# A two-block network on one core: priority for weight splits in two stages, one projection moved ahead by a pair of heads, and norm sums placed behind two of four value blocks

## The chip, the cores and the metric

The kernel runs on one core of one Trainium2 chip. The metric is the device time of one execution in microseconds. Of the kernel before, three executions were timed: 2271.51, 2273.09 and 2273.24 us, median 2273.09 us.

TensorE is called PE here (PEld is its loading of weights), VectorE DVE, ScalarE ACT, GpSimd POOL and SyncE SP. SP issues the loads of weights.

## The reference

512 tokens of width 1024 go through four mixers and two feed-forward parts, all in 32-bit floats:

```python
x = x + lru_mixer(rms_norm(x, g0))     # 2x1536 projections, conv of 4 taps, gates, scan, w_out
x = x + fox_mixer(rms_norm(x, g1))     # 16 heads of 64, causal softmax with a forget term
x = rms_norm(x, final_g)
for i in range(2):                     # hybrid layers
    h = rmsnorm(x, norm_mix[i])
    cb, cc, cu, q, k, v, g, ga, gb = split(h @ w_in[i])
    y_conv = (cb * conv3(cc * cu)) @ w_conv_out[i]
    y_ret = (silu(g) * groupnorm(retention(rotary(q), rotary(k), v))) @ w_ret_out[i]
    x = x + (sigmoid(ga) * y_conv + sigmoid(gb) * y_ret) @ w_o[i]
    h2 = rmsnorm(x, norm_mlp[i])
    x = x + square(relu(h2 @ w_up[i])) @ w_down[i]
out = rms_norm(x, norm_final)
```

## The kernel before, in words

**Products.** Activations lie transposed in SBUF: 8 tiles of 128 features by 512 tokens. Every 32-bit operand is split into a high part H (a cast to fp32r on ACT) and a rest L (a subtraction on DVE), and a product is three matmuls, H·H, H·L and L·H (`mm3`, L279 to L281). A projection of 128 columns (`proj`) is 8 times `mm3`, so 24 matmuls of 512 columns.

**Weights.** `Stream` holds a list of weight items in the order of use. `next()` hands out an item and emits the load and the split of the item two places further on (one, where the current item is a pair of up weights). `_emit` takes a raw buffer (4 of them), issues the load on SP (L119), casts on ACT (L60) and subtracts on DVE (L61) into H and L buffers (3 each). For pairs of up weights `_emit_sums` also forms sums of halves (S1, S2, S4) with DVE additions and splits them into 3 small buffers; one pair of up tiles is then seven products of half width (`pair`) in place of eight.

**Order.** PE runs in the order in which the code is written. The order on ACT, DVE, POOL and SP is made by a planner that plays the program through: of the instructions that it thinks ready, it takes the one traced first. A block `high_priority(300)` counts its instructions as traced 300 instructions earlier, and blocks inside each other add up. The order is fixed in the program; on the chip an engine waits at an instruction that isn't ready, with all that is queued behind it.

**LRU stage (0 to 253.6 us).** For n = 0 to 11: `lru_proj(n)` runs the projections xb and gt; inside a priority block it scales xb by the norm row (xbp, L558), convolves it (one ACT and three DVE instructions, L560 and L562) and splits the result into xcH and xcL. `lru_gates(n-1)` multiplies these with two small weights (psr, psi). For each two n `lru_tail` runs the gate functions on ACT, with four loads of function tables (L585, L595, L599, L610), then the scan (L616), and splits y into yH and yL. `lru_out` (lo) multiplies y with the output weights: one chunk in each of n = 7 to 10, the rest at the end.

**Forgetting attention (fox, to about 552 us).** The heads go in 8 pairs. `fox_q(p)` and `fox_k(p)` project (fq, fk) and split into Tq, Tb, k1 and k2, one buffer each; `fox_sc(p, hh)` computes scores and softmax of one head, `fox_tr` transposes the probabilities (pt) and splits them into ptH and ptL, `fox_pv` multiplies with the values (po), `fox_g` projects the gate (fgt). The loop L869 to L880 runs for p = 1 to 7 the scores of pair p-1 among the projections of pair p; only fq of pair 1 is projected ahead of the loop.

**Retention, in each hybrid layer.** For head 0, PE runs rq and rk together (`proj2`), then the sums of squares over the features (`colsum`, cs) that `first_rows` needs for the norm row r; `rot` rotates q and k with r in the cosines and splits them (rqH to rkL). Four value blocks follow (rv, 24 matmuls of 256 columns each), the transposes of r (rc), the gates (rg; in layer 0 ahead of rc), then the scores (rs).

**Up and down.** After the product with w_o, whose results `PairNorm` turns into x tiles and sums for `pair` (xH, xL, TH, TL), four groups of four pairs of up tiles and eight down tiles (dn) follow. PE starts dn on 6 of 8 tiles aH, aL for two outputs, then does the last two.

Of the kernel before, what the change touches and what calls it, by code (L numbers as in the profile page):

```python
# [15 lines left out]
P = 128  # L16
# [32 lines left out]
class Stream:  # L49


    def __init__(self, tc, raw, hi, lo, items, ahead):
        self.nc, self.raw, self.hi, self.lo = tc.nc, raw, hi, lo
        self.items, self.ahead = items, ahead
        self.done, self.taken = [], 0
        self.sums = self.sraw = None
        self.pooled = 0
# [83 lines left out]
    def prefetch(self, upto):  # L141
        while len(self.done) < min(len(self.items), upto):
            if self.items[len(self.done)][1] is None and self.sums is None:
                return
            self._emit()

# [20 lines left out]
def build(tc, A, out, dbg=None):  # L167
# [3 lines left out]
    with ctx:  # L171
# [39 lines left out]
        for i in range(3):  # L211
            add(f"fox_vf{i}", 0, 3 if i < 2 else 2, 256 + FOX_H)
        add("fox_w_in", 24, KD, P)
        for p in range(1, 8):
            for t in (0, 1, 3):
                add("fox_w_in", t * 8 + p, KD, P)
            if p % 2 == 0:
                for kh in range(2):
                    add("fox_v", (p // 2 - 1) * 2 + kh, 4, 256)
# [294 lines left out]
        with ExitStack() as lc:  # L514
# [34 lines left out]
            st, yH, yL = {}, {}, {}  # L549

            def lru_proj(n):
                ps = proj(psum(f"xb{n}"), W.next()) if n > 1 else (ps0, ps1)[n]
# [105 lines left out]
            lru_out(2, (0, 1, 2), nrm)  # L658
            lru_out(2, (3,), nrm)
            if dbg:  # L660
                for j in range(KD):
                    nc.sync.dma_start(dbg["x1"][:, j], x[:, j])
# [4 lines left out]
        with ExitStack() as lc:  # L667
# [201 lines left out]
            for p in range(1, 8):  # L869
                fox_sc(p - 1, 0)  # L870
                fox_q(p, psq if p == 1 else None)
                fox_sc(p - 1, 1)
                fox_tr(p - 1, 0)
                fox_k(p)
                fox_tr(p - 1, 1)
                fox_pv(p - 1, 0)
                fox_g(p)
                fox_pv(p - 1, 1)
                if p % 2 == 0:
                    fox_v(p // 2)  # L880
# [85 lines left out]
        for li in range(2):  # L966
# [3 lines left out]
            with ExitStack() as lc:  # L970
# [74 lines left out]
                for h in range(RET_H):  # L1045
# [3 lines left out]
                    if h == 0:  # L1049
                        ps, psk = proj2((psum(f"rq{li}_{h}"), psum(f"rk{li}_{h}")), (W.next(), W.next()), [(0, 6), (6, 8)])  # L1050
                        r, r0 = first_rows()
                    else:
                        ps = proj(psum(f"rq{li}_{h}"), W.next())
                    qH, qL = rot("rq", h, ps)
                    if prev:
                        prev = head_o(*prev)
                    kH, kL = rot("rk", h, psk or proj(psum(f"rk{li}_{h}"), W.next()))
                    (h0, l0), (h1, l1) = W.next(), W.next()
                    pss = []
                    for tb in range(4):  # L1060
                        ps = psum(f"rv{li}_{h}_{tb}")[:, :256]
                        cs = slice(tb * P, (tb + 1) * P)
# [59 lines left out]
            with ExitStack() as lc:  # L1122
# [48 lines left out]
                lay = ExitStack()  # L1171
                W.sums = lay.enter_context(tc.tile_pool(name=f"u{li}_s", bufs=3, side="right"))
                W.sraw = lay.enter_context(tc.tile_pool(name=f"u{li}_r", bufs=2, side="right"))
                for j in PAIRS:
# [4 lines left out]
            with ExitStack() as lc:  # L1179
# [6 lines left out]
                for g in range(4):  # L1186
                    ah = []
                    for f in range(0, 8, 2):
# [4 lines left out]
                        for i in range(2):  # L1193
# [5 lines left out]
                            split(aH, aL, t)  # L1199
                            ah.append((aH, aL))  # L1200
                    head = [(W.next(), psum(f"dn{li}_{g}_{j}")) for j in range(2)]
                    for ks in (range(6), range(6, 8)):
# [124 lines left out]
```

## Time and profile before

| | |
|---|---|
| median of three executions | 2273.09 us |
| the profiled execution, its own time | 2273.16 us |
| its span | 2271.4 us |
| PE busy | 2213.1 us (97%) |
| PEld busy | 1908.8 us (84%) |
| DVE busy | 1512.9 us (67%) |
| ACT busy | 1087.9 us (48%) |
| POOL busy | 228.0 us (10%) |

The profiled execution has the time of the median, and 1.8 us of it lie outside the span. Busy time of PE counts each matmul from its start to its modelled end, and these overlap; so idle time is a lower bound on what PE lost, and the distance between the starts of successive matmuls tells more. The granted clock of PE is 1.00 when it runs at 2.4 GHz and 0.50 at 1.2 GHz.

### The profile page before, as it was taken

How to read it: one execution, taken by the hardware profiler on the slowest of the kernel's cores; microseconds unless marked ns; L12 is line 12 of the kernel's file. 1: busy time of each engine (PE TensorE's matmuls, PEld its weight loads, DVE VectorE, ACT ScalarE, POOL GpSimd, SP SyncE). 2: the span in 40 equal slices, each digit the busy share in tenths (PEclk: the TensorE clock that was granted, in tenths of full speed). 3: DMA queues.
4: the chain of work that ended last, by engine and by line, in shares of the span. 5: the costliest groups of instructions: out<-in, count | busy, mean ns of one | idle time of the engine just before them, and what ended most of it. 6: DMA issues, size and time to landing. Idle time of an engine off the chain costs nothing.

```text
span 2271.4 us, 29981 instructions
## 1 busy us (share of the span) xinstructions
PE 2213.1 (97%) x11818; PEld 1908.8 (84%) x11818; DVE 1512.9 (67%) x2316; ACT 1087.9 (48%) x1661; POOL 228.0 (10%) x174
## 2 busy tenths in 40 slices
PE   8899999999999999999899999999999999999998
PEld 6677778887988888888898998988888888898997
DVE  7867877778776445548776785676345548786774
ACT  7667567775655222226443444556222236443443
POOL 0324111110111000000110110211000000110111
PEclk9999999999999999999999999999999999999999
DMA  4223312222232333232333333222333232333331
GB/s 156 72 82 106 93 64 67 74 66 93 78 95 75 102 94 101 93 102 82 97 101 94 111 103 99 91 95 75 102 97 99 93 102 83 103 103 102 96 110 56
DMA packets 62940, 210.40 MB, mean 93 GB/s; under 512 B 6992, under 2 KB 11984, under 8 KB 62800
## 3 DMA queue, kind: packets, MB, share of 16 engines
q1 hardware_dynamic: 59984, 204.43, 28.5%
q10 hardware_dynamic: 2672, 3.81, 0.6%
q8 instruction: 92, 1.51, 0.3%
q14 instruction: 48, 0.39, 0.1%
q0 software_dynamic: 144, 0.26, 0.1%
HBM read 206.37 MB, written 2.10 MB: 92 GB/s over the span
## 4 chain that ended last, share of the span: by engine, by line
PE 87%; DVE 7%; ACT 4%; issue 1%; POOL 0%; DMA 0%; DVEq 0%; SPq 0%; ACTq 0%; POOLq 0%
PE dn L281 5%; PE dn L279 5%; PE dn L280 5%; PE up L281 4%; PE up L279 4%; PE up L280 4%; PE ro L1026 1%; PE gb L279 1%; PE gb L281 1%; PE wo L280 1%; PE cu L281 1%; PE cc L281 1%; PE cb L281 1%; PE wr L281 1%; PE wc L280 1%
## 5 line engine op out<-in xcount | busy, mean ns | idle before, releaser
L60 ACT CAST wh<-wr 128x1024 fp32r<-128x1024 f32 (+1 forms) x335 | 337.6, 1010 | 684.1 <-PE dn L280 117.2
L61 DVE TENSOR_TENSOR wl<-wr,wh 128x1024 fp32r<-128x1024 f32 (+1 forms) x335 | 396.1, 1185 | 43.1 <-ACT wh L60 40.7
L279 PE MATMUL dn<-aH,wh 128*128 128x512 f32 x488 | 190.0, 389 | 0.0
L281 PE MATMUL dn<-aH,wl 128*128 128x512 f32 x488 | 189.9, 389 | 0.0
L280 PE MATMUL dn<-aL,wh 128*128 128x512 f32 x488 | 189.9, 389 | 0.0
L439 POOL TENSOR_TENSOR s_up<-s_up,sz_up 128x256 f32<-128x256 f32 x32 | 61.7, 1929 | 1052.2 <-ACT s_up L437 540.7
L1214 DVE TENSOR_TENSOR x<-dn,x 128x512 f32<-128x512 f32 x61 | 42.0, 688 | 104.6 <-PE dn L281 104.6
L281 PEld LDWEIGHTS dn<-aH,wl 128*128 128x128 f32 x488 | 91.6, 188 | 19.1
L280 PEld LDWEIGHTS dn<-aL,wh 128*128 128x128 f32 x488 | 91.6, 188 | 18.8
L279 PEld LDWEIGHTS dn<-aH,wh 128*128 128x128 f32 x488 | 91.6, 188 | 18.8
L280 PE MATMUL rv<-wl,xH 128*128 128x256 f32 x256 | 73.0, 285 | 0.0
L279 PE MATMUL rv<-wh,xH 128*128 128x256 f32 x256 | 73.0, 285 | 0.0
L281 PE MATMUL rv<-wh,xL 128*128 128x256 f32 x256 | 73.0, 285 | 0.0
L1196 ACT ACTIVATE c_up<-c_up 128x512 f32<-128x512 f32 x64 | 40.3, 633 | 26.3 <-DVE c_up L1195 25.4
L281 PE MATMUL rg<-xH,wl 128*128 128x512 f32 x128 | 49.9, 390 | 0.1
L279 PE MATMUL xb<-xH,wh 128*128 128x512 f32 x96 | 40.5, 422 | 9.8 <-ACT wh L60 9.8
L279 PEld LDWEIGHTS rv<-wh,xH 128*128 128x128 f32 x256 | 49.7, 194 | 0.3
L279 PE MATMUL rg<-xH,wh 128*128 128x512 f32 x128 | 49.9, 390 | 0.0
L280 PEld LDWEIGHTS rv<-wl,xH 128*128 128x128 f32 x256 | 49.6, 194 | 0.4
L279 PE MATMUL gb<-xH,wh 128*128 128x512 f32 x128 | 49.9, 390 | 0.0
L280 PE MATMUL rg<-xL,wh 128*128 128x512 f32 x128 | 49.9, 389 | 0.0
L281 PE MATMUL gb<-xH,wl 128*128 128x512 f32 x128 | 49.8, 389 | 0.0
(1549 smaller groups left out, 6960.3 us busy)
## 6 DMA issues: line engine op xcount, KB each, us to landing
wr<-in_w_in SPq DMA_DIRECT2D x112, 512.0 KB, 3.5
wr<-in_w_down SPq DMA_DIRECT2D x64, 512.0 KB, 3.5
wr<-in_fox_w_in SPq DMA_DIRECT2D x24, 512.0 KB, 3.5
wr<-in_lru_w_in SPq DMA_DIRECT2D x22, 512.0 KB, 3.6
wr<-in_w_v SPq DMA_DIRECT2D x16, 512.0 KB, 3.4
wr<-in_w_ret_out SPq DMA_DIRECT2D x16, 512.0 KB, 3.5
wr<-in_w_conv_out SPq DMA_DIRECT2D x16, 512.0 KB, 3.4
wr<-in_w_o SPq DMA_DIRECT2D x16, 512.0 KB, 3.5
```

What stands on the lines that cost most here:

```text
L60: self.nc.scalar.copy(h, src)
L61: self.nc.vector.tensor_sub(l, src, h.bitcast(F32))
L279: pe.matmul(ps, wH, aH, start=start, stop=False)
L280: pe.matmul(ps, wH, aL, start=False, stop=False)
L281: pe.matmul(ps, wL, aH, start=False, stop=stop)
L439: pool.tensor_add(s5, s5, z)
L1026: pe.matmul(po[i][:, q0:], vp[:, kb, vs], sp_[:, so], start=n == 0, stop=n == 11)
L1196: act.activation(t, t, AF.Square)
L1214: dve.tensor_add(x[:, j], ps, x[:, j])
```

## The change

Nothing is added to or taken from the computation: the instructions are the same, in another order.

1. `Stream.prefetch` emits an item inside `high_priority(first)` when `first` is set. It is 300 from the start of the LRU loop to the end of the LRU stage, and in each hybrid layer from the product with w_o to the end of the first group's four up pairs. In `lru_proj` the call of `next()` for gt stands inside a priority block already.
2. In fox, fk of pair p is projected between the scores of the two heads of pair p-1, the gate ahead of the second transposes, and fq of pair p+1 between the two value products. The items are listed in that order. In the last round (p = 7) no fq follows.
3. In retention, head 0, `first_rows` and both `rot` move behind the second of the four value blocks.

```diff
@@ Stream
+        self.tc, self.first = tc, 0
@@ prefetch
-            self._emit()
+            if self.first:
+                with self.tc.high_priority(self.first):
+                    self._emit()
+            else:
+                self._emit()
@@ items
+        add("fox_w_in", 1, KD, P)
         for p in range(1, 8):
-            for t in (0, 1, 3):
-                add("fox_w_in", t * 8 + p, KD, P)
+            add("fox_w_in", 8 + p, KD, P)
+            add("fox_w_in", 24 + p, KD, P)
+            if p < 7:
+                add("fox_w_in", p + 1, KD, P)
@@ LRU
+            W.first = 300
             def lru_proj(n):
...
             lru_out(2, (3,), nrm)
+            W.first = 0
@@ fox
                 fox_sc(p - 1, 0)
-                fox_q(p, psq if p == 1 else None)
+                fox_q(p, psq)
+                psk = proj(psum(f"fk{p}"), W.next())
                 fox_sc(p - 1, 1)
                 fox_tr(p - 1, 0)
-                fox_k(p)
+                fox_k(p, psk)
+                fox_g(p)
                 fox_tr(p - 1, 1)
                 fox_pv(p - 1, 0)
-                fox_g(p)
+                if p < 7:
+                    psq = proj(psum(f"fq{p + 1}"), W.next())
                 fox_pv(p - 1, 1)
@@ retention
                     if h == 0:
                         ps, psk = proj2(...)
-                        r, r0 = first_rows()
                     else:
-                        ps = proj(psum(f"rq{li}_{h}"), W.next())
-                    qH, qL = rot("rq", h, ps)
-                    if prev:
+                        qH, qL = rot("rq", h, proj(psum(f"rq{li}_{h}"), W.next()))
                         prev = head_o(*prev)
-                    kH, kL = rot("rk", h, psk or proj(psum(f"rk{li}_{h}"), W.next()))
+                        kH, kL = rot("rk", h, proj(psum(f"rk{li}_{h}"), W.next()))
...
                     for tb in range(4):
+                        if h == 0 and tb == 2:
+                            r, r0 = first_rows()
+                            qH, qL = rot("rq", h, psh)
+                            kH, kL = rot("rk", h, psk)
@@ up
+                W.first = 300
                 for j in PAIRS:
...
+                    W.first = 0
                     head = [(W.next(), psum(f"dn{li}_{g}_{j}")) for j in range(2)]
```

## Rows read from the trace of the kernel before

**Rows 1.** Timeline of PE at full clock: start, duration, instruction.

```profile
14.87 0.39 PE L281 MATMUL gt<-xH,wl 128*128 128x512 f32 x1
...
24.39 0.39 PE L281 MATMUL xb<-xH,wl 128*128 128x512 f32 x1
```

**Rows 2.** Windows: stretch, length, busy time (instructions) by engine, PE clock, DMA.

```profile
25.30:214.00 188.70, 172.25 (x717) 137.20 (x716) 142.05 (x173) 127.97 (x177) 53.71 (x29) 0.96 0.28 85
214.00:253.60 39.60, 35.31 (x150) 27.69 (x150) 32.44 (x42) 26.71 (x38) 7.69 (x4) 1.00 0.27 83
297.32:304.14 6.82, 4.69 (x16) 3.93 (x17) 6.12 (x21) 5.10 (x17) 1.28 (x1) 0.50 0.00 0
...
552.00:592.00 40.00, 36.77 (x200) 31.69 (x200) 34.39 (x51) 24.38 (x31) 3.08 (x2) 0.96 0.23 73
...
1069.00:1119.00 50.00, 43.59 (x326) 42.26 (x326) 44.25 (x77) 29.48 (x47) 10.10 (x4) 0.93 0.26 85
1917.00:1967.00 50.00, 44.85 (x355) 43.38 (x354) 46.85 (x81) 31.62 (x50) 8.30 (x4) 1.00 0.28 94
```

**Rows 3.** Waits of PE, whole span: total us, times, longest us.

```profile
PE xb L279 <- ACT wh L60: 9.8, 2, 6.1
PE xb L281 <- DVE wl L61: 5.3, 4, 2.9
PE psr L280 <- DVE xcL L305: 5.0, 4, 1.8
...
PE pt L814 <- ACT pr L802: 4.2, 1, 4.2
PE lo L281 <- DVE wl L61: 3.1, 3, 1.7
...
PE gt L281 <- DVE wl L61: 1.7, 2, 1.2
```

**Rows 4.** Timeline of ACT in the LRU stage.

```profile
81.46 1.28 ACT L595 ACT_TABLE_LOAD   x1
...
89.96 1.03 ACT L60 CAST wh<-wr 128x1024 fp32r<-128x1024 f32 x1
```

**Rows 5.** DVE by line, LRU stage and whole: counts; min/median/max ns.

```profile
L61 DVE TENSOR_TENSOR wl<-wr,wh x45: 414/1217/2311, 25.6 to 252.0; 128x1024 fp32r<-128x1024 f32 x33, 128x256 fp32r<-128x256 f32 x12
...
L562 DVE SCALAR_TENSOR_TENSOR xc<-xbp,vec,xc x36: 741/748/1784, 31.6 to 207.7; 128x512 f32<-128x512 f32 x36
```

**Rows 6.** Timeline of PE, first pair of heads; in brackets idle before, releaser.

```profile
299.45 2.50 PE L814 MATMUL pt<-ident,pr 128*128 128x128 f32 x10 [4.18 <-ACT pr L802]
```

**Rows 7.** Timeline, second transposes of fox's last round and their last split.

```profile
491.04 1.25 PE L814 MATMUL pt<-ident,pr 128*128 128x128 f32 x10
...
495.85 0.69 DVE L822 TENSOR_TENSOR ptL<-pt,ptH 128x512 fp32r<-128x512 f32 x1 [0.18 <-ACT ptH L821]
```

**Rows 8.** Timeline of PE, then of DVE, retention of layer 0, head 0.

```profile
592.10 0.48 PE L279 MATMUL rs<-rqH,rkH 128*128 128x512 f32 x1
...
587.62 0.68 DVE L305 TENSOR_TENSOR rkL<-rark,rkH 128x512 fp32r<-128x512 f32 x1
```

**Rows 9.** Timeline of PE, then of DVE, retention of layer 1, head 0.

```profile
1420.54 0.39 PE L335 MATMUL cs_x<-csl_x,ones 128*128 128x512 f32 x1
...
1432.29 0.60 PE L461 MATMUL rc_s<-ident,r_x 128*128 128x128 f32 x4
...
1443.63 0.39 PE L279 MATMUL rs<-rqH,rkH 128*128 128x512 f32 x1
...
1424.56 0.69 DVE L326 SCALAR_TENSOR_TENSOR r_x<-rst_x,r_x 128x512 f32<-128x512 f32 x1
...
1436.18 0.68 DVE L305 TENSOR_TENSOR rkL<-rark,rkH 128x512 fp32r<-128x512 f32 x1
```

**Rows 10.** Timeline of PE, then of DVE, end of the first up group, layer 0.

```profile
1115.54 0.40 PE L279 MATMUL dn<-aH,wh 128*128 128x512 f32 x1
...
1118.26 1.30 DVE L305 TENSOR_TENSOR aL<-c_up,aH 128x512 fp32r<-128x512 f32 x2 [0.23 <-ACT aH L304]
```

More of the change, by code (lines that the diff above doesn't have):

```diff
@@ L1050, in build @@
                         ps, psk = proj2((psum(f"rq{li}_{h}"), psum(f"rk{li}_{h}")), (W.next(), W.next()), [(0, 6), (6, 8)])
-                        r, r0 = first_rows()
                     else:
-                        ps = proj(psum(f"rq{li}_{h}"), W.next())
-                    qH, qL = rot("rq", h, ps)
-                    if prev:
+                        qH, qL = rot("rq", h, proj(psum(f"rq{li}_{h}"), W.next()))
                         prev = head_o(*prev)
-                    kH, kL = rot("rk", h, psk or proj(psum(f"rk{li}_{h}"), W.next()))
+                        kH, kL = rot("rk", h, proj(psum(f"rk{li}_{h}"), W.next()))
                     (h0, l0), (h1, l1) = W.next(), W.next()
                     pss = []
+                    psh = ps if h == 0 else None
                     for tb in range(4):
+                        if h == 0 and tb == 2:
+                            r, r0 = first_rows()
+                            qH, qL = rot("rq", h, psh)
+                            kH, kL = rot("rk", h, psk)
                         ps = psum(f"rv{li}_{h}_{tb}")[:, :256]
```

## The prediction

> **What bounds the kernel now.** The busy table comes first: PE is busy 97% of the span, so the time is PE's and the other engines count only where PE waits for them. Then I ask how fast PE can go: at full clock 42 matmuls of 512 columns in a row start between 14.87 and 24.39 us, 9.52 / 42 = 0.227 us from one start to the next [rows 1]. The windows by stage then show where PE is slower than that [rows 2]. In the LRU loop, 25.3 to 214.0 us, 717 matmuls would take 717 x 0.227 = 162.8 us and took 188.7: 25.9 us lost. In the end of that stage, 214.0 to 253.6, 150 matmuls would take 34.1 of 39.6: 5.5 lost. Fox loses at its first pair of heads, retention of layer 0 in 552 to 592 (3.2 us idle, clock 0.96), and the two first up groups 6.4 and 5.2 us of idle [rows 2]. Everywhere else PE is never idle for long; nothing is to be gained there.
>
> The list of PE's waits says for whom [rows 3]. In the LRU stage it is mostly the splits of weights: xb waits 9.8 us for casts, of which the 6.1 is the start of the program that no order changes, and 5.3 for the subtractions; gt waits 1.7, lo 3.1. The gates wait 5.0 us in four places for xcL, which is no weight. Beside the waits there is the clock: it was 0.96 in the mean over the LRU loop, so 0.04 x 188.7 = 7.5 us went there [rows 2], after stalls of some 3 us. So a long stall is paid for more than once.
>
> **The change, part by part.** No instruction is added, so each part is worth what it takes from these losses, less what is late next.
>
> *Splits first, LRU.* One stall shows the mechanism: the cast at 89.96 stands on ACT behind three table loads and the functions between them, from 81.46 on [rows 4], and xb starts 3.7 us late for it. With priority the cast goes ahead as soon as its raw data are there; then the subtraction, then the next load on SP (each load waits for a raw buffer that a subtraction frees). What can be gained is 3.7 + 5.3 us of waits of xb, 1.7 of gt, the clock's 7.5, and 2.7 that are left of the 25.9 when these and xcL's 5.0 are taken off (PE filling again after stalls): 20.9 us. I don't take all. DVE is busy 142 of 188.7 us; squeezed into 168 that is 85%, with bursts, and the conv chain that is now behind the splits feeds the gates. Each split put ahead of it costs a DVE instruction of 1.2 us [rows 5] and a cast of 1.03 [rows 4]. The gates already wait at 4 of the 12, and xcL of a later n stood behind the same ACT functions, so once PE arrives earlier it will wait there. I take two thirds: **-14** (bounds -4, the waits for xb's casts alone, and -20.9).
>
> *Splits first, end of LRU.* lo waits 3.1 us for weights, but y of the last two n comes at the end of a chain through the gate functions; PE arriving earlier waits for that. **-0.5** (bounds -3.1 to +3: two splits of 1.2 us put ahead of that chain, and some).
>
> *Fox, first pair.* PE stands 4.18 us for the softmax, since both scores follow each other and the transposes come at once [rows 6]; and from 299.45 to 304.14 it runs at half clock [rows 2], 4.7 us of which half is lost. With fk between the two scores (24 x 0.227 = 5.4 us) the softmax of head 0 is covered; the split of that weight is not on the path, since fk and fq of pair 1 keep their places in the list. 4.2 + 2.35 = **-6.5** (bounds -4.2, -7). Rounds 2 to 6 keep the same distances between scores, transposes and value products, with gate and query in exchanged roles: 0. If their cover were gone, each would cost a part of the 4.18.
>
> *Fox, last round.* There fq is missing, so the second value product follows the first at once. The second transposes end at 492.3, their last split at 496.5 [rows 7], 4.2 us later, of which the first value product, 8 matmuls, covers about 1.4. But k's copies, which stood in between, now come earlier. **+1.5** (bounds 0 and 2.8, or 4.5 if the clock falls for it).
>
> *Retention, layer 0.* The sums wait 3.2 us and 0.04 x 40 = 1.6 go by the clock [rows 2]; behind two value blocks the split sums are ready, so 4.8 us go. What is late next: the scores rs began at 592.10, 3.8 us after rkL ended at 588.30 [rows 8]. PE comes 4.8 us earlier there, and the sums themselves end some 1.7 us later than now (two value blocks of 5.5 us in place of waits of 3.2), with the whole chain of r, cosines, rotations behind them on DVE and POOL: 4.8 + 1.7 - 3.8 = 2.7 us of new wait, less if two weight splits ahead of rkL move up. I take 1.2 of it: **-3.6** (bounds -4.8, -2.1).
>
> *Retention, layer 1.* Nothing waits now. The sums come about 5.8 us later, half of the 11.75 us from 1420.54 to 1432.29. r ended 4.7 us after its sums (1425.25), so it is there in time for the transposes; rkL ended at 1436.86 and is needed at 1443.63, 6.8 us of slack against 5.8 of delay [rows 9]. **+0.5** (bounds 0, +3).
>
> *Splits first, up groups.* DVE is busy 44.25 and 46.85 of 50 us there [rows 2], so priority adds no room: it can only push work behind the start of dn. In layer 0 dn began at 1115.54 and needs its last two tiles 36 matmuls later, at 1123.7; they were ready at 1119.56 [rows 10]: 4.1 us can be pushed, and DVE's 5.7 us of idle in this window hold another 2, since part of them is PE at half clock. Lost now are 6.4 idle and 0.07 x 50 = 3.5 by the clock. I take **-5** (bounds 0, -9.9), and for layer 1, with 5.2 idle and no clock loss, half: **-2.5** (bounds 0, -5.2).
>
> *New stalls.* The planner makes its order anew, and the trace of before can't show where that puts an instruction in the way. I add one stall of the longest kind seen, **+4.2** [rows 6].
>
> Sum: -14 - 0.5 - 6.5 + 1.5 - 3.6 + 0.5 - 5 - 2.5 + 4.2 = -25.9 us. From 2273.16, the profiled execution (which stands at the median, 2273.09), this gives **2247**.
>
> A rule that speaks against the first part: a subtraction of L has two inputs in SBUF, and such instructions pay when POOL reads SBUF at the same time. The row: the same conv instruction takes 0.741 to 1.784 us and a large wl up to 2.311 against 1.217 [rows 5], with POOL busy 53.7 of 188.7 us [rows 2]. The Trainium skill states (SBUF — State Buffer, Who interferes with whom) that the two engines share a port pair as an exclusive lock, and whoever comes second is blocked for the whole instruction. By that rule splits moved into POOL's bursts would cost DVE up to 1 us each; it is the third rival.
>
> **The rivals.**
> *The wait moves to xcL and y.* The conv chain has three ACT and five DVE steps, each of which may now stand behind a split. For it: the gates wait already, DVE has 85% to do. Against: a chain of n has some 16 us, gt, xb, gt of PE, before its gates. The LRU gains nothing: 2247 + 14.5 = 2261.
> *Slower.* The same mechanism, larger: if each of the 11 gates in the loop waits for both splits on DVE (2 x 1.2) and both casts (2 x 1.03), 4.5 x 11 = 49 us, and the clock falls at four of them (half of 6.82 each) [rows 2], 14, against 20.9 + 3.1 saved: +39, with the other parts at -11.4: about 2300; it decides from 3.1 us per gate on ((20.9 + 11.4 + 3.1)/11, the clock left aside). Against it speaks that such a stall frees DVE to catch up.
> *The port, and DVE in the up groups.* 33 large splits at up to 1 us, half of it on PE's path, take 8 of the LRU's gain, and up gains nothing: 2247 + 8 + 7.5 = 2262.
> *Priority does nothing,* since a split that waits for its raw data or for a free H buffer can't go earlier whatever its rank: only PE's own reordering counts, -6.5 + 1.5 - 3.6 + 0.5: 2265.
> *More than forecast.* All named losses go, no new stall: 2273.2 - 20.9 - 3.1 - 7 - 4.8 - 15 = 2222.
>
> **How the numbers follow.** Forecast 0.5, the wait at xcL 0.15, slower 0.07, port 0.08, priority without effect 0.12, more than forecast 0.08. The forecast's own bounds are about 12 us to both sides, since its large terms (14 and 7.5) are known to half. To leave out no more than 2 in 10 the range goes up to 2265, over three of the rivals, and down to 2232. A measurement can tell about 0.2%, 4.5 us. Faster than that: all but the slower case and a part of priority without effect: 0.88; within: 0.05; slower: 0.07.
>
> **What would show it.** In the profile after: xb's waits for wh and wl gone from PE's list, the casts standing among the table loads; the half-clock stretches at 92, 130, 297, 567 and 1106 us gone; no wait of pt at the first pair; a wait of po in fox's last round of some 1.5 us; rs of head 0, layer 0, waiting for rkL about 1 us; sl of the up weights still waited for, but half as much; psr's wait for xcL larger than 5.0. Wrong would be the prediction if psr's waits pass 20 us, or if xb still waits for splits.

## The result and the profile after

The changed kernel takes 2285.9 us (median), the kernel before 2273.0 beside it: ratio 1.0059, 95% interval 1.0046 to 1.0072. It is slower by 0.6%, where the prediction said 2247 us and faster with 0.88. The profiled execution has a span of 2284.0 us against 2271.4, so 12.6 us have to be found.

PE has the same 11818 matmuls and the same busy time (page of after):

```profile
PE 2213.7 (97%) x11818; PEld 1905.6 (83%) x11818; DVE 1512.1 (66%) x2316; ACT 1088.9 (48%) x1663; POOL 226.8 (10%) x174
```

The stages say where the time went. The table is read from PE's timeline, from the first matmul of one stage's first product to that of the next (fq starts fox, sc its attention, rq retention, ro is head 0's output, wo to dn holds the first up group). The runs described further down stand in the same table, since the comparison by stage is the argument. Each row is one profiled execution, which can lie some us off its kernel's median (that of e3_ret is the fastest of its ten, that of e10_ret_one the slowest):

| kernel | fq starts | sc to rq | rq to ro, layer 0 | wo to dn, layer 0 | wo to dn, layer 1 | span |
|---|---|---|---|---|---|---|
| before | 253.5 | 261.3 | 47.5 | 93.6 | 90.0 | 2271.4 |
| after | 252.6 | 268.8 | 53.5 | 93.6 | 89.9 | 2284.0 |
| e1_priority | 253.2 | 261.1 | 47.6 | 93.4 | 89.8 | 2270.6 |
| e2_fox | 252.1 | 268.8 | 48.1 | 89.8 | 91.4 | 2275.7 |
| e4_fox_hold | 251.3 | 261.0 | 48.2 | 92.5 | 92.6 | 2271.1 |
| e5_round1 | 252.1 | 257.8 | 47.2 | 89.9 | 91.1 | 2263.6 |
| e3_ret | 251.1 | 260.6 | 53.6 | 91.3 | 91.1 | 2273.2 |
| e8_ret_sin | 252.3 | 261.7 | 50.2 | 91.3 | 89.8 | 2270.9 |
| e10_ret_one | 255.8 | 261.3 | 46.3 | 92.6 | 91.2 | 2272.8 |
| e11_both | 252.3 | 258.2 | 46.2 | 92.8 | 91.3 | 2266.5 |
| e6_lru | 254.7 | 261.8 | 47.3 | 92.4 | 91.3 | 2273.0 |
| e9_bufs | 264.6 | 260.8 | 48.6 | 90.2 | 89.4 | 2281.4 |
| e12_lru2 | 252.2 | 261.3 | 47.5 | 93.5 | 89.6 | 2269.9 |
| e13_lru2_dve | 246.1 | 261.7 | 47.4 | 93.8 | 90.0 | 2264.6 |
| e14_best | 252.2 | 257.8 | 48.3 | 90.0 | 91.2 | 2265.0 |
| e15_all | 246.4 | 257.8 | 47.2 | 91.1 | 89.9 | 2257.9 |
| e16_dve | 243.4 | 262.0 | 47.3 | 92.6 | 91.6 | 2262.4 |
| e17_round1_dve | 243.3 | 257.8 | 47.0 | 91.3 | 91.4 | 2256.3 |
| e18_nopool | 247.2 | 257.8 | 48.2 | 92.8 | 91.3 | 2263.0 |

After minus before: -0.9 to the end of the LRU, +7.5 in fox, +6.0 in retention of layer 0, 0.0 and -0.1 in the up groups, and nothing elsewhere. Some columns also show their own unsteadiness. Kernels with the LRU code of before (before, e2 to e5, e8, e10, e11) end that stage between 251.1 and 255.8. The first up group of layer 0, whose code only the priority touches, takes 89.8 to 90.0 us without a stretch at half clock, 91.1 to 92.8 with one of 3.4 us and 93.4 to 93.8 with one of 6.8 us (e9_bufs, which has other buffers, apart). So a difference of some 4 us between two kernels is read from the stage that was changed, not from the total.

In the LRU the waits of PE, which answer to [rows 3], are nearly what they were; the 6.2 us of psr are no sign of the change, since e2_fox, with the LRU code of before, has 6.4 (after, waits of PE from 25 to 253 us: total us, times, longest):

```profile
PE psr L288 <- DVE xcL L313: 6.2, 4, 2.5
PE xb L289 <- DVE wl L62: 4.9, 4, 2.9
PE xb L287 <- ACT wh L61: 3.9, 1, 3.9
PE lo L289 <- DVE wl L62: 3.2, 3, 1.7
```

The cast that answers to [rows 4] still stands behind the three table loads (after, timeline of ACT):

```profile
82.95 1.28 ACT L605 ACT_TABLE_LOAD   x1
...
91.44 1.03 ACT L61 CAST wh<-wr 128x1024 fp32r<-128x1024 f32 x1
```

Its raw data had landed at 73.3 us, and the product that last read its H buffer (xb, three weight items earlier) ended at 81.4. So neither held it back on the chip for the last 10 us: its place in ACT's fixed order did.

The windows answer to [rows 2]: the LRU loop again at clock 0.96, then the two up groups, at the same distance from dn as the windows of before, with the same busy time and clock:

```profile
25.30:214.00 188.70, 172.76 (x721) 137.91 (x722) 143.16 (x175) 128.79 (x178) 55.99 (x30) 0.96 0.27 85
...
1081.70:1131.70 50.00, 43.35 (x326) 42.02 (x325) 44.38 (x77) 29.40 (x47) 10.11 (x4) 0.93 0.25 85
1929.60:1979.60 50.00, 44.89 (x355) 43.41 (x354) 46.63 (x81) 31.52 (x50) 8.32 (x4) 1.00 0.28 94
```

In fox the single wait of 4.18 us [rows 6] has gone, and seven others of about 1.3 us have come (after, waits of PE from 286 to 560, then from 558 to 625 in retention):

```profile
PE pt L825 <- DVE mxs L814: 9.3, 7, 1.4
PE po L846 <- ACT ptH L832: 1.0, 1, 1.0
```

```profile
PE rs L287 <- ACT rkH L312: 6.3, 1, 6.3
PE rg L287 <- DVE rsm_n L330: 1.2, 1, 1.2
PE cs_n L343 <- DVE csl_n L313: 0.7, 1, 0.7
PE cs_n L342 <- ACT csh_n L312: 0.5, 1, 0.5
```

Where the seven come from is seen on ACT in the second round (after, timeline of ACT):

```profile
329.55 0.62 ACT L777 CAST Tb<-qf 64x512 fp32r<-64x512 f32 x1
330.08 0.61 ACT L788 CAST k<-kf 64x512 fp32r<-64x512 f32 x1
330.71 0.27 ACT L832 CAST ptH<-pt 128x128 fp32r<-128x128 f32 x1
330.88 0.62 ACT L789 CAST k<-kf 64x512 fp32r<-64x512 f32 x1
331.40 1.22 ACT L832 CAST ptH<-pt 128x256 fp32r<-128x256 f32 x3
332.64 0.58 ACT L813 ACTIVATE pr<-sc,mxs 128x384 f32<-128x384 f32 x1
```

PE stands for the end of that softmax in the middle of the second transposes (after, timeline of PE):

```profile
332.92 0.49 PE L825 MATMUL pt<-ident,pr 128*128 128x128 f32 x3
334.74 0.52 PE L825 MATMUL pt<-ident,pr 128*128 128x128 f32 x3 [1.33 <-DVE mxs L814]
```

The copies of the keys (L788, L789) stand ahead of the second head's exponential (L813). In the kernel before they came behind it (before, ACT, same round):

```profile
330.74 0.58 ACT L802 ACTIVATE pr<-sc,mxs 128x384 f32<-128x384 f32 x1
...
334.81 0.62 ACT L777 CAST k<-kf 64x512 fp32r<-64x512 f32 x1
...
336.75 0.62 ACT L778 CAST k<-kf 64x512 fp32r<-64x512 f32 x1
```

Before, the product fk stood behind the first transposes, so the keys couldn't be copied earlier. Now fk is done before the second scores, k is free as soon as these end, and the copies, ready sooner, go first.

### The profile page after: what moved, and what is told of

It is laid out like the page before. It is cut to its first block, busy times and chain, and to the rows that moved or that the text cites. A ratio compares the mean times of both kernels' runs of the same rounds, so it can differ in the third digit from the quotient of the medians.

```text
span 2284.0 us, 29968 instructions
## 1 busy us (share of the span) xinstructions
PE 2213.7 (97%) x11818; PEld 1905.6 (83%) x11818; DVE 1512.1 (66%) x2316; ACT 1088.9 (48%) x1663; POOL 226.8 (10%) x174
## 4 chain that ended last, share of the span: by engine, by line
PE 80%; DVE 12%; ACT 4%; issue 2%; DMA 1%; POOL 0%; SPq 0%; DVEq 0%; ACTq 0%; POOLq 0%
PE dn L289 5%; PE dn L287 5%; PE dn L288 5%; PE up L289 4%; PE up L287 4%; PE up L288 4%; DVE wl L62 2%; PE ro L1040 1%; PE gb L289 1%; PE gb L288 1%; PE wc L288 1%; PE wc L287 1%; PE ga L288 1%; PE ga L287 1%; PE cu L288 1%
## 5 line engine op out<-in xcount | busy, mean ns | idle before, releaser
L289 PEld LDWEIGHTS dn<-aH,wl 128*128 128x128 f32 x488 | 91.6, 188 | 19.1
L288 PEld LDWEIGHTS dn<-aL,wh 128*128 128x128 f32 x488 | 91.6, 188 | 18.8
L287 PEld LDWEIGHTS dn<-aH,wh 128*128 128x128 f32 x488 | 91.6, 188 | 18.8
L288 PE MATMUL gb<-xL,wh 128*128 128x512 f32 x128 | 49.8, 389 | 0.0
L287 PE MATMUL wr<-yrH,wh 128*128 128x512 f32 x128 | 49.8, 389 | 0.0
L288 PE MATMUL wr<-yrL,wh 128*128 128x512 f32 x128 | 49.8, 389 | 0.0
```

The source lines that it names most:

```text
L287: pe.matmul(ps, wH, aH, start=start, stop=False)
L288: pe.matmul(ps, wH, aL, start=False, stop=False)
L289: pe.matmul(ps, wL, aH, start=False, stop=stop)
```

## The experiments

### The three parts alone

**e1_priority** keeps the program of before and adds only the priority.

```diff
-            self._emit()
+            with self.tc.high_priority(self.first): self._emit()
...
-            st, yH, yL = {}, {}, {}
+            st, yH, yL, W.first = {}, {}, {}, 300
...
```

Other lines of the edit set it back to 0 after the LRU, and set and reset it again around the first up group of each layer.

> The kernel before with the priority of the splits alone. The prediction's sum gave this part -14 us at the LRU's rounds, -0.5 at its end and -7.5 at the up groups, so 2251 us. The theory after reading the trace of the changed kernel: a split waits for its H buffer, which comes free when the product three chunks earlier ends, and the sigmoid work that stands ahead of it on ScalarE was put there because it was ready sooner; the priority then changes hardly any order, and the time stays at 2273 us, within 2 us.

2272.0 us, ratio 0.9992 (0.9983 to 1.0002): no difference. The instruction lists say why. Against the kernel before, ACT's order of 1586 instructions (table loads left out) differs in one place, in the LRU, and DVE's in one place too (the subtraction of the same split):

```
@@ -78,6 +78,6 @@
 L560 ACTIVATE xc_650<-xbp_318,vec 128x512
 L621 CAST yH_526<-hs_521 128x512
+L60 CAST wh_693<-wr_692 128x1024
 L304 CAST xcH_655<-xc_650 128x512
-L60 CAST wh_693<-wr_692 128x1024
```

A priority of 2000 in place of 300, in a kernel that was built and not run, gives the same two lists. So the cast of [rows 4] keeps its place behind the table loads, and in the up groups nothing moves at all.

**e2_fox** and **e3_ret** take the new fox loop (list of weights and loop) and the moved sums (both layers) alone, each as the hunks of the diff above have it.

> The kernel before with the new order of the fox loop alone. The prediction gave it -6.5 us for the first pair and +1.5 for the last round, so 2268 us. The theory after reading the changed kernel's trace: 7 rounds lose 1.8 us each in front of the second transposes and the first pair wins its 4.2 us of wait and its half clock back, about +7.5 us together, so 2280 us.

2278.2 us, ratio 1.0022 (1.0012 to 1.0031); fox takes 268.8 us as in the changed kernel, and PE waits 9.4 us in seven places at pt.

> The kernel before with the norm sums of both retention layers behind two of the four value blocks, alone. The prediction gave it -3.6 us in layer 0 and +0.5 in layer 1, so 2270 us. The theory after reading the changed kernel's trace: the chain from the sums to the rotated keys starts 10.2 us later and the scores rs wait 6.4 us for rkH at a clock that falls to half, +6.0 us, all in layer 0: 2279 us.

2278.4 us, ratio 1.0022 (1.0013 to 1.0031); rq to ro takes 53.6 us. The 10.2 us in this expectation are wrong: they count fox's delay too. From the start of rq the sums end 3.6 us later than before (19.5 against 15.9 us), and rkL 8.8 us later (45.0 against 36.2): the chain behind the sums has grown by 5.2. In layer 1 rq to gb takes 154.9 us in before, after and here: nothing.

### Fox: whose place is it

**e4_fox_hold** is e2_fox with the keys' copies issued behind the second head's last exponential.

```diff
-                fox_k(p, psk)
+                with tc.issue_after(fox_sc.exp):
+                    fox_k(p, psk)
...
```

> The new order of the fox loop alone, with ScalarE's four copies of the keys (0.62 us each) issued behind the last exponential of the second head's scores. Theory: the stall before the second transposes comes from these copies, which stand ahead of that head's exponentials because the key product is done before its scores; held back, the 7 stalls of 1.8 us go and the first pair's gain stays: 2280 - 12.8 = 2267 us. Rival: the stall comes from what else is queued there (the query's copies, the gate's split); then it stays at 2278 to 2280 us. Second rival: the held copies come too late for the next pair's scores, and the stall moves there at the same size.

The stalls shrink from 1.3 to 0.3 us each, so the copies are most of what stood in the way; what the remaining 0.3 wait for was not tried (e4_fox_hold, waits of PE, 288 to 549):

```profile
PE po L838 <- ACT ptH L824: 2.7, 1, 2.7
PE pt L817 <- DVE pr L807: 1.9, 7, 0.3
```

But the time is 2276.0 us (ratio 1.0015, 1.0005 to 1.0024), not 2267, and fox takes 261.0 us, as before. The lengths of the rounds, from one pair's first score to the next pair's, give the account. A round without stall takes 24.7 us (36.2 with a value product), and one with a projection less 24.7 - 24 x 0.227 = 19.2. Before: the first round 26.75, two projections, 7.5 lost; the others nothing. After: 27.41 with three, 2.7 lost; five rounds of 26.5 or 38.0, 1.83 lost in each; the last 22.39 with two, 3.2 lost: 15.0 in all, 7.5 more than before. e4_fox_hold: 26.04, 1.35 lost; five times 0.45; the last 22.78, 3.5 lost: 7.1. With the copies out of the way the new order is worth nothing: the 6.15 us that it wins in the first round it pays in the last, where po now waits 2.7 us, and in the five between. The median lies 3 us above that of before, while the two profiled spans agree to 0.3 us: the profiled execution is the second fastest of ten, which range from 2272.1 to 2280.0 us, with a mean granted clock of 0.994 in the two fastest and 0.991 in the two slowest. Where that clock falls in the slower ones was not traced.

**e5_round1** uses the new order in the first of the seven rounds alone.

```diff
+                psk = proj(psum("fk1"), W.next()) if p == 1 else None
                 fox_sc(p - 1, 1)
                 fox_tr(p - 1, 0)
-                fox_k(p)
+                fox_k(p, psk)
+                if p == 1:
+                    fox_g(p)
...
```

> The kernel before with the new order in the first of the seven fox rounds alone (the product of pair 1's keys ahead of pair 0's second scores, the gate's behind its first transposes). Theory: the first pair's wait of 4.2 us and the 1.7 us of its half clock go, the round loses 1.5 to 1.8 us in front of the second transposes, as each of the seven did, and the other six rounds stay as they were: -4.5 us, 2268 us. If the gain of the first pair is not separable from the order of the later rounds: 2272 us or more.

2267.0 us, ratio 0.9970 (0.9960 to 0.9980). Fox takes 3.5 us less than before; the round is 23.21 us long, 4.0 lost in place of 7.5 (two waits, and no half clock behind them):

```profile
PE pt L814 <- DVE mxs L803: 1.4, 1, 1.4
PE po L835 <- ACT ptH L821: 0.9, 1, 0.9
```

The rest of the 6.5 us lies in stages that it doesn't touch (the LRU's end, the first up group of layer 0): the stretches at half clock that before has at 130 and 1106 us are missing there, and one of 3.4 us has come in layer 1. As far as these runs show, that part is luck; what the order itself is worth is the 3.5. **e11_both**, below, holds the copies in this round too: pt then waits 0.3 us and po 2.7, and the round takes 23.67 us, no gain.

### Retention: why 6 us and not 1

**e8_ret_sin** moves the sums of layer 0 alone and issues the sine work behind the first row's exponential.

```diff
+                        if h == 0 and li == 0 and tb == 2:
+                            r, r0 = first_rows()
...
                         rsqrt_row(r, s2, None, tn, "n2")
+                        with tc.issue_after(rsqrt_row.exp):
+                            trig_sin()
```

> The kernel before with the norm sums of retention layer 0 alone moved behind two value blocks, and with the rotation's sine work on ScalarE issued behind the first row's exponential. Theory: what made the wait of rs 6.4 us instead of the 1.2 that the prediction gave is that the sine work and two more table loads (1.28 us each) stand between the sums and the row; behind it, the chain from the sums to the keys is as long as in the kernel before and rs waits 1 to 2 us, without the fall to half clock: 2272 to 2274 us, against the 2278 us of the move alone. Rival: the wait comes from the sums' later start, and rs waits 5 us or more as before: 2277 to 2279 us.

2273.2 us, ratio 1.0000 (0.9991 to 1.0009); rq to ro is 50.2 us against 53.6 for the move and 47.5 before. In the kernel before the sines came behind the row (before, timeline of ACT):

```profile
568.75 0.63 ACT L319 ACTIVATE rst_n<-s2n 128x512 f32<-128x512 f32 x1 [2.97 <-DVE s2n L1007]
...
570.06 1.28 ACT L505 ACT_TABLE_LOAD   x1
```

In e3_ret (timeline of ACT) the table that is loaded for the row at 566.69 is pushed out by the sines' own at 567.98, and logarithm and exponential then each load one:

```profile
566.69 1.28 ACT L317 ACT_TABLE_LOAD   x1
567.98 1.28 ACT L505 ACT_TABLE_LOAD   x1
569.27 0.63 ACT L505 ACTIVATE sind<-cosd 64x512 f32<-64x512 f32 x1
...
571.87 1.28 ACT L319 ACT_TABLE_LOAD   x1
573.16 0.63 ACT L319 ACTIVATE rst_n<-s2n 128x512 f32<-128x512 f32 x1
573.82 1.28 ACT L323 ACT_TABLE_LOAD   x1
575.11 0.63 ACT L323 ACTIVATE r_b<-rst_n 128x512 f32<-128x512 f32 x1
```

With the sines behind it, one load serves both, and the row comes at once (e8_ret_sin, timeline of ACT):

```profile
568.96 1.28 ACT L317 ACT_TABLE_LOAD   x1
571.50 0.63 ACT L319 ACTIVATE rst_n<-s2n 128x512 f32<-128x512 f32 x1 [1.26 <-DVE s2n L1008]
572.16 0.63 ACT L323 ACTIVATE r_b<-rst_n 128x512 f32<-128x512 f32 x1
572.81 1.28 ACT L506 ACT_TABLE_LOAD   x1
```

So 3.4 of the 6.1 us are the sines and the two loads. The other 2.7 remain: rs still waits 2.6 + 0.4 us, and still falls to half clock behind it.

**e10_ret_one** puts the sums behind one value block instead of two, otherwise as e8_ret_sin.

```diff
-                        if h == 0 and li == 0 and tb == 2:
+                        if h == 0 and li == 0 and tb == 1:
```

> The kernel before with the norm sums of retention layer 0 alone behind one of the four value blocks instead of two, and the sine work behind the first row's exponential. Theory: the price of the move is the later start of the chain from the sums to the keys, which has 3.8 us of slack; behind one block (2.8 us of PE) the sums end about as late as in the kernel before, rs waits for nothing, and of the sums' own waits of 3.6 us some 1.7 stay: -1.5 to -3 us, 2270 to 2271.5 us. Rival: the chain is late for other reasons than its start, and rs waits 2 us or more here too: 2273 us.

2270.7 us, ratio 0.9991 (0.9982 to 1.0000); rq to ro is 46.3 us, 1.2 less than before, and rs waits 1.5 us for rkL. The start of the sums is thus what the remaining 2.7 us hung on. **e11_both** joins it to the first fox round, with that round's copies held:

```diff
+                if p == 1:
+                    with tc.issue_after(fox_sc.exp):
+                        fox_k(p, psk)
...
```

> The new order in the first fox round alone, with that round's copies of the keys held behind the second head's exponentials, and the norm sums of layer 0 behind one value block with the sine work behind the row's exponential. Theory: the first round alone gave -6.5 us; its own stall in front of the second transposes shrinks from 1.5 to 0.4 us, and the sums give 1.5 to 3: 2262 to 2265 us. If the parts are not additive because a half clock comes back elsewhere: 2267 us.

2269.2 us, ratio 0.9982 (0.9973 to 0.9991): a smaller gain than that of e5_round1 alone. Its fox and retention are 3.1 and 1.3 us shorter than before, but the up group of layer 0 takes 92.8 us against 89.9 in e5_round1, that is half clock again.

### The LRU: what priority did not reach

**e6_lru** puts the split ahead by hand: the sigmoid work is traced one step later, and its first table switch issued behind the cast of the next xb weights.

```diff
-                    with tc.issue_after(last):
+                    with tc.issue_after(last), tc.issue_after(cast or last):
                         silu = act.activation(s["gt"], s["gt"], AF.Silu).ins
...
```

> The kernel before with the LRU's sigmoid work of two chunks traced one step later and its first table switch on ScalarE issued behind the split of the next chunk's xb weights: order by hand instead of priority. Theory: the splits were late because ScalarE's queue holds five activations and three table loads (9 us) between a split and its H buffer's release, and a priority does not reach past work that is ready sooner; with the split put ahead by hand the wait of 3.8 + 1.7 us at 91 us and the half clock behind it go: -6 to -9 us, 2264 to 2267 us. Rival: the tail's chain is then the late one, and the waits come back at the gates (psr) or at the output products (yH): 2272 us.

2274.6 us, ratio 1.0006 (0.9996 to 1.0016). xb no longer waits for a cast; the wait moved on by one projection, to gt (e6_lru, waits of PE, 25 to 254):

```profile
PE gt L282 <- DVE wl L121: 5.7, 4, 1.7
PE gt L280 <- ACT wh L120: 5.5, 2, 2.9
```

**e9_bufs** gives the halves 4 buffers instead of 3 (wlo as whi below), the raw weights 2 instead of 4, and takes weights three items ahead.

```diff
-        wraw = ctx.enter_context(tc.tile_pool(name="wraw", bufs=4))
-        whi = ctx.enter_context(tc.tile_pool(name="whi", bufs=3))
+        wraw = ctx.enter_context(tc.tile_pool(name="wraw", bufs=2))
+        whi = ctx.enter_context(tc.tile_pool(name="whi", bufs=4))
...
-        W = Stream(tc, wraw, whi, wlo, items, 2)
+        W = Stream(tc, wraw, whi, wlo, items, 3)
```

> The kernel before with 4 buffers for the H and L halves instead of 3, paid for by 2 for the raw weights instead of 4, and weights taken three items ahead instead of two. Theory: if the H buffer's release is what keeps a split from standing ahead of the sigmoid work, one buffer more lets each split be ready one product sooner; the LRU's waits for weights (wh, wl) shrink by most of their 7 to 9 us, 2264 to 2268 us. Rival: with two raw buffers the transfers start later and the projections wait for them instead: 2275 us or slower.

2286.0 us, ratio 1.0057 (1.0042 to 1.0072). Waits for weights fell from 14.3 to 9.5 us, but those for xc and y grew from 6 to 17 (e9_bufs, waits of PE, 25 to 264):

```profile
PE psr L280 <- DVE xcL L305: 8.7, 4, 2.7
PE lo L279 <- ACT yH L621: 5.7, 1, 5.7
```

So splits that come earlier seem to push the convolution and the scan behind them, though two raw buffers fewer were not tried apart from the rest. **e12_lru2** cuts the sigmoid work in two pieces, with a split ahead of each:

```diff
+                    with tc.issue_after(last), tc.issue_after(cast[0] if cast else last):
                         silu = act.activation(s["gt"], s["gt"], AF.Silu).ins
...
+                    with tc.issue_after(exp), tc.issue_after(cast[1] if cast else exp):
                         act.activation(s["sq"], s["tau"], AF.Sqrt, scale=-1.0)
...
```

> The kernel before with the LRU's sigmoid work of two chunks traced behind the next chunk's gates; its first table switch on ScalarE stands behind the split of the next xb weights and the switch to the square root behind the split of the next gt weights. Theory: each wait for weights in this stage comes from three table loads and their functions issued in one piece; cut in pieces, the waits of xb (5.5 us at 91) and those that the hand order of xb alone moved to gt (3.0 + 1.9 and 2.8 + 1.7 us) both go: -5 to -9 us, 2264 to 2268 us. Rival: VectorE's part of the same work is late then, and the waits come back at the gates or at the output products: 2272 to 2275 us.

2271.4 us, ratio 0.9991 (0.9982 to 1.0000). ACT no longer holds PE up much, DVE does: gt waits 7.2 us for wl, longest 2.2. Ahead of one of those wl, DVE and POOL look like this (e12_lru2, timelines):

```profile
75.93 3.42 DVE L563 SCALAR_TENSOR_TENSOR xc<-xbp,vec,xc 128x512 f32<-128x512 f32 x2
79.27 0.68 DVE L569 TENSOR_TENSOR gt<-gt,r_n 128x512 f32<-128x512 f32 x1
79.87 1.69 DVE L121 TENSOR_TENSOR wl<-wr,wh 128x1024 fp32r<-128x1024 f32 x1
```

```profile
74.98 3.82 POOL L619 TENSOR_TENSOR hs<-hs,gt 128x512 f32<-128x512 f32 x2 [4.89 <-DVE hs L617]
78.77 1.72 POOL L623 TENSOR_TENSOR yL<-hs,yH 128x512 fp32r<-128x512 f32 x1
80.45 2.26 POOL L588 TENSOR_TENSOR ig<-ig,xc 128x512 f32<-128x512 f32 x1
```

Two steps of the convolution take 3.42 us where [rows 5] has 0.75 for one. **e13_lru2_dve** therefore puts the products hs and yL of all chunks on DVE, and **e16_dve** does that alone, in the order of before.

```diff
-                    eng = dve if n >= LRU_B - 2 else pool
+                    eng = dve
```

> The order by hand of the kernel e12_lru2, and the two products per chunk at the tail of the LRU (h times gate, and the L half of y), which POOL computed for ten of the twelve chunks, on VectorE. Theory: what is left of the waits there (gt for its wl, 2.0 to 2.4 us at 81.62, 96.39 and 111.17) is VectorE held up while POOL works: in the burst of POOL from 74.98 to 84.42 three instructions of the convolution take 1.67 to 1.77 us instead of 0.75 and the split in front of gt 1.69 instead of 1.22, 3.4 us together; without POOL's bursts these waits go, -3 to -6 us against e12_lru2: 2265 to 2268 us. Rival: VectorE pays 0.69 us for each of the 20 products that it takes over, as much as it wins, and the waits stay: 2270 to 2274 us.

2266.4 us, ratio 0.9974 (0.9963 to 0.9984).

> The kernel before with the tail's two products on VectorE for all twelve chunks, nothing else. Theory: the LRU stage is held back by VectorE while POOL works, and the order of the splits on ScalarE matters little (1.5 us): most of the 5 to 6 us comes without any change of order, 2267 to 2269 us. Rival: it is the order by hand that makes VectorE's freed time count; alone, the products on VectorE give 0 to 1 us: 2271 to 2273 us.

2263.1 us, ratio 0.9958 (0.9945 to 0.9972): one line without any order wins at least as much as the order by hand with it. The LRU ends at 243.4 us against 253.5; the two stretches at half clock that before has there, 6.8 us long each, are gone, and PE's waits from 25 us to the stage's end fell from 20.4 to 14.8 us. The loop runs at clock 1.00 (e16_dve, window; [rows 2] has 0.96 and 53.71 us of POOL), and the wait for the cast is gone from the list:

```profile
25.30:214.00 188.70, 177.42 (x762) 141.23 (x761) 149.12 (x201) 137.99 (x190) 28.45 (x12) 1.00 0.29 94
```

**e18_nopool** takes the last product of the LRU off POOL as well, beside the fox round of e5_round1; **e17_round1_dve** is the same without that step.

```diff
-                    pool.tensor_mul(ig, ig, s["xc"])
+                    dve.tensor_mul(ig, ig, s["xc"])
```

> The LRU tail's two products on VectorE for all chunks and the new order in the first fox round alone, without any order of the splits. Theory: the products alone gave -9.5 us, the round -6.5, and they add up: 2256 to 2258 us. Rival: the order by hand and the round won with the products because a half clock fell away with either; then 2260 us, as with the order by hand.

> As e17_round1_dve, and the product of the input gate with the convolved chunk on VectorE too, so that POOL computes none of the LRU's products. Theory: each of the 12 products left on POOL still holds VectorE up for one instruction, by up to 1 us; without them 1 to 3 us more than e17_round1_dve. Rival: VectorE, busy 149 of 188.7 us by then, is paid for with 0.69 us each and nothing is won or 2 us are lost.

e17_round1_dve: 2259.0 us, ratio 0.9936 (0.9923 to 0.9950), between what its theory and its rival named. e18_nopool: 2262.7 us, ratio 0.9955 (0.9942 to 0.9969), slower than e17 by 3.7. The same DVE group of the convolution in before, e16_dve and e18_nopool (groups of DVE, 25 to 254 us: busy us, mean ns | idle before):

```profile
L562 DVE SCALAR_TENSOR_TENSOR xc<-xbp,vec,xc 128x512 f32<-128x512 f32 x36 | 35.3, 986 | 0.5 <-ACT xc L560 0.2
```

```profile
L562 DVE SCALAR_TENSOR_TENSOR xc<-xbp,vec,xc 128x512 f32<-128x512 f32 x36 | 29.7, 833 | 0.4
```

```profile
L562 DVE SCALAR_TENSOR_TENSOR xc<-xbp,vec,xc 128x512 f32<-128x512 f32 x36 | 26.6, 747 | 0.7 <-ACT xc L560 0.6
```

With POOL idle none of the 36 takes over 0.753 us: POOL is what slows them. The Trainium skill states (SBUF — State Buffer, Who interferes with whom) that the two engines share a port pair as an exclusive lock; these runs agree, as far as the slowing goes. But e18_nopool, with POOL idle, is not the fastest kernel. Its LRU ends 3.9 us later than that of e17, though PE's waits there are no longer (14.5 us against 15.3): it has three stretches at half clock of 3.4 us each, 5.1 us lost, where e17 has none. Whether the last product on DVE costs anything beside these is not shown.

e16_dve saves DVE about 36 x (0.986 - 0.833) = 5.5 us here, 2.7 on the large wl, 3.7 on xcL and 1.1 on the scan, and pays 20 x 0.68 = 13.6 for the products: DVE takes over 20 products and its busy time from 25.3 us to the end of the stage stays what it was (174.4 us before, 173.6). What also changed is the chain to y: POOL took 1.88 and 1.96 us for a product, DVE 0.68. Shorter steps on DVE, a shorter chain to y, and no half clock behind the waits can each have won PE's time; which counts most was not told apart.

**e14_best** and **e15_all** join the fox round with the order by hand, without and with the products on DVE.

> The new order in the first fox round alone and the LRU order of e12_lru2, together. Theory: the parts lie in different stages and add up: -6.5 and -1.5 us, 2264 to 2266 us. Rival: the LRU's gain of 1.5 us is within what the phase of the half-clock stretches does from kernel to kernel, and nothing is added: 2267 us.

2266.7 us, ratio 0.9973 (0.9963 to 0.9983): the order by hand adds nothing to e5_round1.

> The order of e12_lru2, the tail's two products on VectorE as in e13_lru2_dve, and the new order in the first fox round alone, together. Theory: the LRU stage's gain (217.3 to 209.6 us of stage, 5 to 6 us of time) and the first fox round's (6.5 us) lie in different stages and add up: 2260 to 2262 us. Rival: the half-clock stretches that each removes come back in a later stage, as far as 3 us: 2264 us.

2259.9 us, ratio 0.9945 (0.9931 to 0.9958): the two stages' gains add up. The lowest median is that of e17_round1_dve, 14.7 us below the kernel before and 27 below the changed one; e15_all, 0.9 us above it, is not told apart from it.

## Why the prediction was wrong

| part | predicted | measured (profiled executions) |
|---|---|---|
| splits first, LRU and its end | -14.5 | -0.9, within what the same code varies |
| fox | -5.0 | +7.5 |
| retention, layer 0 | -3.6 | +6.0 |
| retention, layer 1 | +0.5 | 0.0 |
| splits first, up groups | -7.5 | -0.1 |
| new stalls | +4.2 | in fox's 7.5 |
| sum | -25.9 | +12.6 |

**The LRU.** The step that failed is "With priority the cast goes ahead as soon as its raw data are there". The stall of [rows 4] was read rightly, its remedy wrongly: with priority the cast ran at 91.4 us, 18 us after its raw data and 10 after its H buffer was free, and of the whole order one place on ACT and one on DVE changed. The rival "priority does nothing" named that; it got 0.12, and its 2265 failed with the two parts that it kept. That a rank orders only what is ready together fits the two lists, but how the planner set each instruction's readiness no run shows. The bound also was too good: ordered by hand the splits gave 1.7 us or nothing, since what holds the weights back there is DVE, with POOL's products in its way and in its chain. The paragraph on the port said the first half of that and priced it against the change alone, not as a loss of the kernel before. The terms of the up groups failed by the same step: -7.5 was taken, and priority moved no instruction there (-0.1).

**Fox.** The first pair's term was right in kind: the wait of 4.18 and its half clock went. Without the new stall it would have been -6.15 (e4_fox_hold: 7.5 lost before, 1.35 there), near the -6.5. In the changed kernel it was -4.8. The step that failed is "Rounds 2 to 6 keep the same distances ... 0": distances on PE were kept, but not what is free when. fk's results became ready one step earlier, and four copies of 0.62 us moved into the middle of the softmax on ACT: five rounds at 1.83. The sentence behind it ("If their cover were gone, each would cost a part") had the mechanism and no price. The last round lost 3.2, where 1.5 was taken and 2.8 was the bound without the clock; 1.83 of it is the stall of every round, so what is its own is about 1.4.

**Retention, layer 0.** The step is "2.7 us of new wait ... I take 1.2": rs waited 6.3. The delay of the sums was taken as 1.7, where its own figures, 5.5 less 3.2, give 2.3; it was 3.6, because the sums still waited 1.2 of their 3.2 us and two value blocks took 5.75 us; and the chain behind them was taken as fixed, while the sine work, which before came behind the row, slid in front of it. The half clock then followed the stall: 0.94 in the mean from rq to ro, where it was 0.96.

**New stalls** was a lump of one stall of the longest kind. One stall per round, at a third of the size, came to twice as much.

Three smaller figures of the working are off without bearing on the outcome: the slower rival decides from 3.2 us per gate on, not 3.1 (35.4 / 11); the two half-clock stretches of the LRU loop lose half of 2 x 6.83, 6.8 us, not 7.5; and the conv chain has two ACT steps, not three.

Of the signs given in advance, the wait of po in the last round came (1.0 us, 1.5 named). psr's longer wait for xcL came too (6.2 us), but e2_fox has it without the priority. Of the half-clock stretches, the one at 297 us went; those at 92 and 130 stayed (at 91 and 132, with a third at 40), and those at 567 and 1106 stand at 600 and 1119. The rest did not come: pt waits more, not less, rs waits 6.3 us and not 1, the casts don't stand among the table loads, and the up weights (sl) are waited for as before. That xb still waits for splits was named as what would refute the prediction.

## What to carry to other kernels

When a product is moved earlier, list what its results set free on the other engines, and which instruction that was last in a queue is now ready first: in an engine that works in order it goes ahead of the work the matmuls wait for, and in a loop it does so every round. A priority is worth what it changes in the instruction lists, so compare the lists before counting on it. And before ordering work around a busy VectorE, look at what GpSimd does beside it: the line that moves two products was worth 10 us of its stage here, the best reordering 3.5 of its own.

## What was not expected of the hardware

With no product of the LRU on POOL, 36 convolution steps on DVE took 0.740 to 0.753 us; with POOL at work the same steps took up to 1.784. POOL needed 1.88 us for a product of 128x512 that DVE does in 0.68. In e3_ret a function table loaded ahead of its use, at 566.69 us, was lost to another function's load at 567.98, and the two functions that it was meant for then loaded one each, 1.28 us apiece.
